# TensorE, ScalarE and VectorE in the text's order through the middle of a hybrid HGRN2/GLA trunk

## Chip, cores and metric

The kernel runs on one core of a Trainium2 chip. The metric is the device time of one execution in microseconds; the profile adds the span from the first to the last instruction, the instructions of each engine and the transfers.

## The reference

One layer over a sequence of 1024 tokens and 1024 channels, float32, batch 1. A conditioning vector gives a shift, a scale and a gate by `c_act @ ada_w`; the normalised input is modulated and projected once:

```python
h = rms_norm(x, norm_w[l]) * (1.0 + scale[:, None, :]) + shift[:, None, :]
proj = h @ w_in[l]
hq, hf, hi, hz, gq, gk, gv, gz, ga, mg = jnp.split(proj, IN_OFFSETS, axis=-1)
y_h = hgrn2_branch(hq, hf, hi, hz, lb_all[l], hgrn_norm_w[l])
y_g = gla_branch(gq, gk, gv, gz, ga, gla_alpha_w[l], gla_alpha_b[l], gla_norm_w[l])
u_h = y_h @ w_branch[l, 0]
u_g = y_g @ w_branch[l, 1]
merged = mg[:, :, 0] * u_h + mg[:, :, 1] * u_g
x = x + gate[:, None, :] * (merged @ w_out[l])
```

Here `mg` has been put through a sigmoid. Both branches are gated linear recurrences over time, `S_t = diag(a_t) S_{t-1} + k_t v_t^T` and `o_t = S_t^T q_t`: HGRN2 with 8 heads (keys and values 128 wide), GLA with 4 heads (keys 128 wide, values 256). Each branch output is normalised and multiplied by a SiLU gate. A final RMS norm closes.

## The kernel before

Every large product is made of three matmuls: each float32 operand is split into a rounded part `hi` and a rest `lo`, and hi·hi, hi·lo and lo·hi are added in PSUM. A split is one ScalarE cast (L211, L202, L1270, L1293) and one VectorE subtraction behind it (L212, L203, L1271, L1294), both on 128x1024.

The text goes through these stages. The first part (conditioning, normalisation, the first half of a first group of projections) is already in the text's order. `front()` finishes the first group. Then `stream.go()` runs a list of 62 jobs: 14 jobs `Vjob` that make the GLA values (L1899, two half products by a seven-product scheme), gate and key jobs of GLA (`Feat`, L607), 14 `Vjob` for the HGRN values, two more `Feat`, and 24 `Feat` for HGRN, three to a head: q, f and z. `last_stages()` and `out_stage()` follow with the mixing gates (`mg`), the branch and output products (L1351, L1528).

A job is cut into units of six matmuls 128x512: a `Vjob` has 4, a `Feat` has 8. After each unit `go()` calls `ahead`, which loads and splits the weights of the next jobs if slots are free, and `weave`, which advances two side tracks:

- `side` holds the attention heads, one after another. A head is a generator that yields how many units to wait before its next piece; the wait is divided by `PACE` 1.08 for GLA and `PACE_H` 1.15 for HGRN.
- `back` holds preparation for later: GLA decay rates (`alpha_side`), sums of weights (`v_sums`, `prepare` with its four additions L1195, L1197, L1199, L1201 per block) and the output gate (`gate_side`, seven accumulations L1072).

One head's pieces, in the text's order: VectorE builds scaled copies of q and k (L658 to L661, called the X block below; ScalarE copies q at L657); two or three units later TensorE makes a first set of scores (L665); VectorE scales q, k and the decays (L667 to L670), masks the scores into `blk` (L676, L679, L680, L681 for each half), then L682, L684, L693 and L694, which the next scores need (L698). Behind L698 stand L700 to L704, five masked copies (L739, L740, L742) and two growth steps of L726, L727, L729; after some units the scores L756, L762, L767 and their growth step, the transposes L791, the state updates (L813 on TensorE, L817 and L819 on VectorE) and the outputs (L832, L834), each half of which is squared on ScalarE (L1002 for GLA, L1123 for HGRN) and scaled on VectorE (L1003, L1124). A GLA head ends with an inverse root: two matmul pairs (L979, L980), a logarithm (L981), an exponential (L982) and eight products on VectorE (L1017). The next head starts when the one before it has ended, an HGRN head not earlier than five units after its f job.

At the end of a job its PSUM result is taken out: SiLU by ScalarE and VectorE (L967, L968) for q, z and the GLA gates, two sigmoids and three VectorE operations (L1102 to L1104) for f. Near the end of `go()` two hooks prepare the next stage; one, `begin_2`, stands four units before the last job's end and splits the factors (L1270, L1271) and one pair of weights (L1293, L1294).

What sets the order of the work: a scheduler takes the instructions that the text emits. On each engine it issues the instruction that stands earliest in the text among those that it holds to be ready in a model of the machine; an instruction whose inputs are late is passed by later ones. `keep_in_program_order` pins single instructions, `high_priority` (used with `EVICT_FIRST` around the taking out of a `Vjob`) moves some forward, and `manual_schedule(engines=...)` makes the named engines issue everything emitted inside it in the text's order. Before the change it is open only for the first part, as `order`. SyncE and GpSimd, which issue the transfers, are left to the scheduler everywhere. SBUF tiles come from 46 slots (`Slots`), handed out as the text is traced.

```python
    def go(self, loads=2, preps=1):
        for i, job in enumerate(self.jobs):
            self.ahead(i, loads + 2 * job.more, 0)
            for u, _ in enumerate(job.run()):
                if job.calls(u):
                    self.ahead(i, loads + 2 * job.more, preps + (job.more if u else 0))
                if (n - i, u) in self.hooks:
                    self.hooks[n - i, u]()
                self.weave(1)
```

Of the kernel before, what the change touches and what calls it, by code (L numbers as in the profile page):

```python
# [89 lines left out]
def hybrid_trunk_kernel(  # L90
# [805 lines left out]
    stream = Stream()  # L896
# [1039 lines left out]
    def front():  # L1936
        alpha = [alpha_half(half) for half in range(2)]
        for i, _ in enumerate(first_group()):
            if i < 10 and i % 2 == 0:
                next(alpha[0], None)  # L1940
            if i == 15:
                for _ in make_ga(1):
                    pass
                load_wq(0, 0)
                load_wq(1, 0)
            elif i in (16, 17, 18, 20, 22):
                next(alpha[1], None)
            elif i == 19:
                stream.ahead(0, 0, 0)
        for n, z in enumerate(("12", "22")):  # L1950
            xq[z] = [hT[1, 2 * n + kk] for kk in range(2)]
        stream.back.append([alpha_side((2, 3)), 72, 1, 0])
        stream.back.append([v_sums(), 2, 1, 0])
        stream.back.append([prepare(), 4, 1, 0])
        stream.back.append([gate_side(), 4, 1, 0])
# [1 line left out]
    stream.hooks[2, 0] = begin  # L1957
    stream.hooks[1, 4] = begin_2
    front()
    stream.go()  # L1960
    S.free(*h_hi, *h_lo)
    lent = [dtile() for _ in range(2)]
    R.lend([pd for pds in lent[::-1] for pd in pds])
# [31 lines left out]
```

## Time and profile before

| what | value |
|---|---|
| time, median of 3 runs | 1176.97 us (1176.68 to 1178.28) |
| profiled execution: time, span | 1178.0 us, 1176.2 us |
| TensorE busy | 1156.2 us, 98% of the span, 8137 matmuls |
| VectorE, ScalarE, GpSimd busy | 849.6 us (72%), 589.5 us (50%), 125.0 us (11%) |
| granted TensorE clock | 0.996 |
| `Vjob` matmuls L1899 | 672, mean 393 ns |
| `Feat` matmuls L607 | 1632, mean 395 ns |

A matmul's duration in the profile is longer than the step from one to the next, because matmuls overlap; the idle time of TensorE tells whether it waits. Times in rows are counted from the span's start. In the span's order `go()` reaches from about 111 us (first L1899) to about 778 us (last L607).

### The profile page before, as it was taken

What the parts mean: (1) busy time and instruction counts of PE and PEld (TensorE: products, weight loads), DVE (VectorE), ACT (ScalarE), POOL (GpSimd) and SP (SyncE); (2) the same over time, 40 slices, a digit from 0 to 9 for tenths busy, and PEclk for the clock granted to TensorE, in tenths of its full rate; (3) what the DMA queues carried; (4) which work ended last, traced back from release to release, by engine and by line L of the source; (5) the groups of instructions that cost most, each with busy time, mean ns of one, the idle gap of its engine ahead of it and who ended that gap; (6) DMA issues with size and microseconds to landing.
All of it is one profiled execution on the core that took longest, in us unless ns stands there. A gap on an engine that the chain in (4) does not pass through costs nothing.

```text
span 1176.2 us, 20432 instructions
## 1 busy us (share of the span) xinstructions
PE 1156.2 (98%) x8137; PEld 953.1 (81%) x8137; DVE 849.6 (72%) x1347; ACT 589.5 (50%) x903; POOL 125.0 (11%) x261
## 2 busy tenths in 40 slices
PE   7999999999999999999999999999999999999997
PEld 5777888888888788888888878888888888888886
DVE  4754778567665946897897798795643866988994
ACT  4675464663465535433433425567543644534654
POOL 4121111000100212111111010001110000000000
PEclk8999999999999999999999999999999999999999
DMA  9846445255675856565555453247699846434523
GB/s 319 279 149 233 161 170 189 77 165 171 207 260 177 279 189 201 171 203 173 174 184 188 134 205 112 91 162 241 196 314 298 274 156 215 130 108 162 187 90 134
DMA packets 150802, 221.44 MB, mean 188 GB/s; under 512 B 9052, under 2 KB 107410, under 8 KB 150707
## 3 DMA queue, kind: packets, MB, share of 16 engines
q1 hardware_dynamic: 132114, 158.37, 43.2%
q0 software_dynamic: 18544, 61.76, 13.6%
q8 instruction: 64, 1.05, 0.4%
q14 instruction: 32, 0.25, 0.1%
q10 hardware_dynamic: 48, 0.01, 0.0%
HBM read 154.57 MB, written 65.54 MB: 187 GB/s over the span
## 4 chain that ended last, share of the span: by engine, by line
PE 64%; issue 25%; DVE 4%; POOL 3%; DMA 2%; ACT 1%; SPq 0%; POOLq 0%; DVEq 0%; ACTq 0%
PE pd L607 16%; PE pd L1899 11%; PE pd L1351 9%; PE sc_ps L1351 5%; PE pm L1351 4%; PE pd L1528 3%; PE pd L396 3%; PE sc_ps L1528 2%; PE pm L832 1%; PE pm L1528 1%; POOL ws L1203 1%; PE sc_ps L396 1%; PE pm L834 1%; PE pm L813 1%; DMA b<-qk 1%
## 5 line engine op out<-in xcount | busy, mean ns | idle before, releaser
L607 PE MATMUL pd<-b,b 128*128 128x512 f32 x1632 | 391.1, 395 | 0.2 <-DVE b L212 0.2
L607 PEld LDWEIGHTS pd<-b,b 128*128 128x128 f32 x1632 | 302.1, 188 | 64.3 <-DVE b L212 0.6
L1351 PE MATMUL pd<-b,b 128*128 128x512 f32 x720 | 169.8, 390 | 0.1
L1899 PE MATMUL pd<-b,b 128*128 128x512 f32 x672 | 157.5, 393 | 2.6 <-ACT b L211 1.2
L1351 PEld LDWEIGHTS pd<-b,b 128*128 128x128 f32 x720 | 134.8, 188 | 28.5 <-ACT pd L1334 0.5
L1899 PEld LDWEIGHTS pd<-b,b 128*128 128x128 f32 x672 | 125.3, 188 | 30.5 <-ACT b L211 1.6
L212 DVE TENSOR_TENSOR b<-b,b 128x1024 fp32r<-128x1024 f32 x78 | 94.3, 1221 | 35.0 <-ACT b L211 34.7
L1294 DVE TENSOR_TENSOR b<-b,b 128x1024 fp32r<-128x1024 f32 x56 | 68.4, 1225 | 68.5 <-ACT b L1293 54.4
L1293 ACT CAST b<-b 128x1024 fp32r<-128x1024 f32 x56 | 58.5, 1049 | 69.5 <-PE pm L1351 17.0
L211 ACT CAST b<-b 128x1024 fp32r<-128x1024 f32 x78 | 79.8, 1047 | 12.1 <-DMA v<-b 3.9
L1351 PE MATMUL sc_ps<-b,b 128*128 128x512 f32 x324 | 77.2, 390 | 0.0
L1270 ACT CAST b<-b 128x1024 fp32r<-128x1024 f32 x48 | 49.7, 1049 | 46.5 <-PE pd L1351 16.0
L1351 PE MATMUL pm<-b,b 128*128 128x512 f32 x300 | 71.1, 389 | 0.0
L1351 PEld LDWEIGHTS sc_ps<-b,b 128*128 128x128 f32 x324 | 60.7, 188 | 12.6
L1271 DVE TENSOR_TENSOR b<-b,b 128x1024 fp32r<-128x1024 f32 x48 | 58.0, 1226 | 17.0 <-ACT b L1270 11.5
L1351 PEld LDWEIGHTS pm<-b,b 128*128 128x128 f32 x300 | 56.3, 188 | 11.7
L718 ACT COPY xb<-b 128x512 f32<-128x512 f32 x48 | 29.7, 621 | 55.8 <-DVE b L700 18.9
L1203 POOL DMA_DIRECT2D ws<-b x64 | 34.8, 545 | 190.6 <-DVE b L1195 118.7
L203 DVE TENSOR_TENSOR b<-b,b 128x1024 fp32r<-128x1024 f32 (+1 forms) x37 | 35.9, 984 | 26.4 <-ACT b L202 26.3
L396 PE MATMUL pd<-b,b 128*128 128x512 f32 x192 | 51.9, 403 | 0.5 <-ACT b L202 0.4
L832 PE MATMUL pm<-scT,b 128*128 128x128 f32 x256 | 46.9, 275 | 0.5 <-DVE b L819 0.5
L396 PEld LDWEIGHTS pd<-b,b 128*128 128x128 f32 x192 | 34.3, 188 | 11.6 <-ACT b L202 1.5
(316 smaller groups left out, 1713.3 us busy)
## 6 DMA issues: line engine op xcount, KB each, us to landing
b<-in_w_in_dram SPq DMA_DIRECT2D x72, 512.0 KB, 4.1
ws<-b POOLq DMA_DIRECT2D x64, 256.0 KB, 3.6
b<-ws SPq DMA_DIRECT2D x32, 512.0 KB, 4.6
b<-in_x_dram SPq DMA_DIRECT2D x16, 512.0 KB, 4.2
b<-in_ada_w_dram SPq DMA_DIRECT2D x32, 256.0 KB, 6.5
v<-b POOLq DMA_DIRECT2D x32, 256.0 KB, 4.3
b<-v SPq DMA_DIRECT2D x16, 512.0 KB, 5.0
b<-fx SPq DMA_DIRECT2D x16, 512.0 KB, 4.6
```

The lines of the kernel that those rows point to most:

```text
L211: held(nc.scalar.copy(hi, src))
L212: nc.vector.tensor_sub(lo, src, hi.bitcast(F32))
L396: nc.tensor.matmul(accs[f], wg(a, d, f), b[d][:, half * 512:half * 512 + 512], start=(d == 0 and n == 0), stop=(d == KT - 1 and n == 2))
L607: nc.tensor.matmul(ps[th][0:w, :], a[:, k, 0:w], b[:, th * 512:(th + 1) * 512], start=(k == 0 and n == 0), stop=(k == KT - 1 and n == 2))
L832: nc.tensor.matmul(o, vch(ch)[:, vh * P:(vh + 1) * P], scT[:, ch, :], start=True, stop=(ch == 0))
L1270: nc.scalar.copy(hi, src)
L1271: nc.vector.tensor_sub(lo, src, hi.bitcast(F32))
L1293: nc.scalar.copy(hi, t)
L1294: nc.vector.tensor_sub(lo, t, hi.bitcast(F32))
L1351: nc.tensor.matmul(o, a[:, sl], c, start=(p in (1, 5) and kt == 0 and n == 0), stop=(kt == 3 and n == 2), skip_group_check=True)
L1528: nc.tensor.matmul(o, a, b, start=(p in (1, 5) and kt == 0 and n == 0), stop=(kt == 3 and n == 2), skip_group_check=True)
L1899: nc.tensor.matmul(st.bank[i], x_, w_, start=(p in (1, 5) and kk == 0 and a == 0 and n == 0), stop=(kk == 1 and a == 1 and n == 2), skip_g ...
```

## The change

The call of `stream.go()` is put into a `manual_schedule` region for the three compute engines. Everything that `go()` emits on them, jobs, splits, heads and back track, is issued there in the text's order. The set of instructions, their tiles and slots, and the freedom of SyncE and GpSimd stay as they are; where the region's instructions fall among those emitted before and after it is still the scheduler's choice.

```diff
@@ -1957,7 +1957,8 @@
     stream.hooks[2, 0] = begin
     stream.hooks[1, 4] = begin_2
     front()
-    stream.go()
+    with tc.manual_schedule(engines={mybir.EngineType.PE, mybir.EngineType.Activation, mybir.EngineType.DVE}):
+        stream.go()
     S.free(*h_hi, *h_lo)
```

## The prediction, made before the changed kernel ran

> **What bounds the kernel now.** I read the busy time of the engines in windows first, then TensorE's order in time, then VectorE's beside it, and last the groups for single durations. The window rows give busy us of TensorE, its weight loads, VectorE, ScalarE and GpSimd; the second row is the stretch that the change covers.
>
> ```profile
> 473.00:784.00 311.00, 309.92 (x3206) 257.65 (x3206) 259.37 (x504) 134.95 (x245) 33.48 (x62) 1.00 0.52 165
> 106.00:784.00 678.00, 673.44 (x5821) 559.93 (x5820) 514.81 (x905) 325.52 (x516) 80.60 (x149) 1.00 0.55 178
> ```
>
> TensorE idles 678.00 - 673.44 = 4.56 us there. Nothing but TensorE's waits can be won, so 4.56 us is the whole possible gain. VectorE is at 514.81/678 = 76%, in the HGRN part at 259.37/311 = 83%; ScalarE is at 48%.
>
> Is TensorE's order the text's already? The timeline of HGRN head 2:
>
> ```profile
> 550.74 8.46 PE L607 MATMUL pd<-b,b 128*128 128x512 f32 x36
> 559.12 1.31 PE L665 MATMUL sc_ps<-xb,b 128*32 128x80 f32 x64
> 560.37 5.73 PE L607 MATMUL pd<-b,b 128*128 128x512 f32 x24
> 566.03 0.89 PE L698 MATMUL sc_ps<-xb,b 128*32 128x48 f32 x64
> 566.85 9.81 PE L607 MATMUL pd<-b,b 128*128 128x512 f32 x42
> ```
>
> Six matmuls are a unit. The text's count: a head starts 5 units after its f job; the yields 3, 5 and 4+3, each unit taking off 1.15, put L665 two units later, L698 four after L665, L756 seven after L698, and the next L665 follows L832 by six. The rows show 36, 24 and 42 matmuls: 6, 4 and 7 units. TensorE stands in the text's order now, so for it the edit changes nothing but waits; what changes is the order of ScalarE and VectorE.
>
> **The change part by part.** No instruction, byte or tile is added or removed, and none moves to another queue. SyncE and GpSimd stay the scheduler's; their loads and stores are hidden by work one or more jobs ahead, and would cost their lateness if that lead were gone. What goes is that VectorE and ScalarE pass an instruction whose input is late. What stands behind it now waits with it: on VectorE the X block and the L212 of the next job's split, and behind these TensorE's L665, L698 and the next job's first matmuls. ScalarE I cost at nothing: its idle half covers the changed order, and if that cover is gone one cast of about the length of a split's VectorE part (1.2 us, row L212 below) shows. The lost priority for taking out `Vjob` results I also cost at nothing: in the text that copy stands right behind its matmuls, and another bank is being filled.
>
> VectorE in head 2 (start, duration), and the square on ScalarE that its second L1124 waits for:
>
> ```profile
> 549.81 0.65 DVE L658 TENSOR_TENSOR xb<-b,b 128x256 f32<-128x256 f32 x1
> 550.35 0.75 DVE L1124 SCALAR_TENSOR_TENSOR b<-pm,vec,b 128x512 f32<-128x512 f32 x1
> ...
> 552.30 0.73 DVE L1124 SCALAR_TENSOR_TENSOR b<-pm,vec,b 128x512 f32<-128x512 f32 x1
> ...
> 562.26 0.30 DVE L679 COPY_PREDICATED blk<-mask,sc_ps 128x96 f32<-128x96 int32 x1
> 562.43 0.28 DVE L676 TENSOR_TENSOR blk<-sc_ps,eye 128x128 f32<-128x128 f32 x1
> ...
> 564.23 0.43 DVE L694 TENSOR_TENSOR xb<-xb,tot 128x256 f32<-128x256 f32 x1
> ...
> 567.24 0.27 DVE L701 TENSOR_TENSOR tot<-tot 128x64 f32<-128x64 f32 x1
> 567.54 0.28 DVE L702 TENSOR_TENSOR tot<-tot 128x64 f32<-128x64 f32 x1
> ...
> 572.50 1.22 DVE L212 TENSOR_TENSOR b<-b,b 128x1024 fp32r<-128x1024 f32 x1
> 573.64 0.69 DVE L726 TENSOR_TENSOR b<-b,tot 128x512 f32<-128x512 f32 x1
> ```
>
> ```profile
> 551.02 0.60 ACT L1123 ACTIVATE b<-pm 128x512 f32<-128x512 f32 x1 [1.19 <-PE pm L834]
> ```
>
> - *Fill lost.* Between 549.81 and 552.30 VectorE did L658, L659 and L667 around the first L1124: 2.49 - 0.66 = 1.83 us of later work in time that the text's order leaves idle. There the second L1124 starts at 551.02 + 0.60 + 0.06 = 551.7 instead of 552.30, so 1.83 - 0.6 = 1.2 us is net loss.
> - *Neighbours that depend.* L676 of one half follows L679 of the other after 0.17 us; L702, which reads what L701 wrote, follows after 0.30 us at the same length. The text puts L676, L679, L680, L681 of a half in a row, each on the last one's result: 6 such gaps at 0.13 to 0.15 us are 0.9 us, three more (L659-L660, L684-L693, L693-L694) 0.4 us. By L694 that is 1.3 us, and with three gaps among the masked copies 1.75 us by L212.
> - *Growth before the split.* In the text L212 stands behind the second growth step's L726 and L729, in the trace ahead of them: 0.7 us.
>
> One place of the Trainium skill speaks against the second item. VectorE: DVE Perf Modes, section "The DRAIN you can't avoid", says that eight chained copies took the same time with a semaphore after each as without, so that dependence costs nothing extra. The rows here disagree (0.17 against 0.30 us); by the page the sum would lose the second item, and I go by the rows.
>
> Deadlines: L694 is due at L698, the L212 at the first lo·hi matmul of the job, four matmuls after its start. L694 ends at 564.66, due 566.03: 1.37 us spare, 1.2 + 1.3 = 2.5 needed. L212 ends at 573.72; the job starts 30 matmuls after 566.85, at (9.81 - 0.28)/42 = 0.227 us each at 573.65, due 574.55: 0.83 spare, 1.2 + 1.75 + 0.7 = 3.65 needed. The second contains the first: head 2 loses 2.8 us. The other heads, by their L212 and the same matmuls (the row of head 4; heads lie 42.76 us apart):
>
> ```profile
> 487.69 1.22 DVE L212 TENSOR_TENSOR b<-b,b 128x1024 fp32r<-128x1024 f32 x1
> ...
> 527.82 1.23 DVE L212 TENSOR_TENSOR b<-b,b 128x1024 fp32r<-128x1024 f32 x1
> ...
> 614.11 1.22 DVE L212 TENSOR_TENSOR b<-b,b 128x1024 fp32r<-128x1024 f32 x1
> ...
> 657.37 1.22 DVE L212 TENSOR_TENSOR b<-b,b 128x1024 fp32r<-128x1024 f32 x1
> ```
>
> ```profile
> 652.37 9.81 PE L607 MATMUL pd<-b,b 128*128 128x512 f32 x42
> ```
>
> Due times 489.0, 531.8, 617.3 and 660.1; spare 0.1, 2.7, 2.0 and 1.5. Heads 1, 3 and 4 lose 0.9, 1.7 and 2.2. Head 0 follows a GLA head, has no L1124 in its way and has its growth step done before L212: only 1.75 needed, loss 1.65. In heads 5 and 6 the accumulations of the gate, which now slip in early, go back to their place behind L212; I take these two at no change (bounds 0 and 2.8 each).
>
> Head 7: `begin_2` emits three splits of 1.13 us on VectorE (3.4 us) right before the X block; the trace has them after it.
>
> ```profile
> 772.12 0.67 DVE L661 TENSOR_TENSOR xb<-xb,b 128x256 f32<-128x256 f32 x1
> ```
>
> ```profile
> 775.85 1.31 PE L665 MATMUL sc_ps<-xb,b 128*32 128x80 f32 x64
> ```
>
> Spare 3.06 us, needed 3.4 + 1.2: loss 1.6. HGRN sum: 1.65 + 0.9 + 2.8 + 1.7 + 2.2 + 1.6 = 10.85 us.
>
> GLA heads. Head 1's X block runs 50 us ahead of its place now, as filling:
>
> ```profile
> 199.68 0.64 DVE L658 TENSOR_TENSOR xb<-b,b 128x256 f32<-128x256 f32 x1 [4.13 <-PE sc_ps L762]
> ...
> 248.22 2.77 DVE L1017 TENSOR_TENSOR b<-b,b 128x256 f32<-128x256 f32 x8 [4.16 <-ACT b L982]
> 250.90 1.28 DVE L968 TENSOR_TENSOR b<-b,pd 128x512 f32<-128x512 f32 x2
> ```
>
> ```profile
> 252.00 1.31 PE L665 MATMUL sc_ps<-xb,b 128*32 128x80 f32 x64
> ```
>
> ```profile
> L659 DVE TENSOR_TENSOR xb<-b,b 128x512 f32<-128x512 f32 x12 | 10.4, 867 | 0.0
> L661 DVE TENSOR_TENSOR xb<-xb,b 128x256 f32<-128x256 f32 x12 | 7.7, 643 | 0.2
> ```
>
> In the text it stands behind the last L1017 and the job's L968, which end at 252.18, and takes 0.64 + 0.87 + 0.87 + 0.64 = 3.0 us: ready at 255.2, L665 due at 252.00, loss 3.2 us. Heads 2 and 3 have the same tail in the values stage; between nothing and 3.2 each I take 2.5, near the measured one. Sum 8.2 us. Head 0 and the first values stage I take at nothing: their VectorE work has no L1017 ahead of it and their splits are emitted a job and a half early; a single X block late would be 3.0.
>
> The waits there now (4.56 us) I leave in: most are at splits whose place in the text is late too. Sum: 10.85 + 8.2 = 19.05 us on the profiled execution's 1178.0 (span 1176.2 and 1.8 around it), 1197.0; the median lies 1.03 lower, so 1196.0.
>
> **The rivals.** *Faster.* Passing is also what makes the present waits: a filler takes VectorE just before the instruction that TensorE waits for. If the text's pacing suffices and two thirds of the 4.56 us go, the time is about 1174; it decides if the X blocks and L212 come earlier than my sums say, by more than the spares. Against it: the spares are 0.1 to 2.7 us, and every filler of head 2 was work that is due anyway. *No change.* Waits trade places: 1177. *Dependence is free.* Without the second item heads 0, 1 and 3 fit, 2 and 4 lose 1.1 and 0.4, head 7 1.6: 3.1 + 8.2 = 11.3, 1188. This is what the page's rule gives; the rows speak against it. *Blocking spreads.* ScalarE's casts wait behind logarithms and squares too, the heads 5 and 6 and the first stage lose as much as head 2, and GLA heads lose twice: 8 x 2.8 + 3 x 6.4 = 41.6 at the end (1218.6), some 1211 in the middle. For it: an in-order engine adds up its waits; against it: ScalarE is half idle, VectorE regains its lag between L756 and L832.
>
> **How the numbers follow.** Likeliest, 1189 to 1204: 0.45, at 1196. Dependence free, 1180 to 1189: 0.15. Spreading, above 1204: 0.16. No change, within 0.2% (2.35 us, about what a measurement of this kernel can tell): 0.12. Faster, at least 1172.4 by the bound: 0.12. For 8 in 10 the range goes from 1176, which leaves out the faster case and a part of no change, to 1210 with the lower half of spreading. Slower 0.76, same 0.12, faster 0.12.
>
> **What would show it.** Right: TensorE's rows keep 36, 24 and 42 matmuls between the scores; its waits grow at L665 (from VectorE L661), at L698 (L694) and at job starts (L212), most in heads 2 and 4 and in GLA heads 1 to 3; L676 to L681 stand in a row at 0.3 us; L658 of GLA head 1 comes after 250. Wrong: TensorE idle at or under 4.56 us; or waits mostly from ScalarE or from transfers; or another count of matmuls between the scores.

## The result and the profile after

The changed kernel took 1218.09 us (1216.71 to 1218.55), the kernel before 1177.62 us on the same chip: ratio of the means 1.0335, 95% interval 1.0308 to 1.0361. It is 40.5 us slower, where 19 were predicted. The profiled execution took 1218.55 us. Below, a time stands for the median of undisturbed executions, and e4_first and e9_wide have no undisturbed trace.

The core's span and granted clock, then the two window rows that answer to those of before (busy us of TensorE, weight loads, VectorE, ScalarE, GpSimd, then granted clock, DMA share, GB/s):

```profile
core 0: 1216.8 us, clock 0.986
```

```profile
473.00:784.00 311.00, 301.11 (x2901) 246.75 (x2901) 254.56 (x475) 118.39 (x218) 39.67 (x72) 0.99 0.52 167
106.00:784.00 678.00, 647.73 (x5398) 532.43 (x5397) 498.71 (x848) 290.81 (x469) 80.07 (x147) 0.98 0.52 169
```

TensorE now idles 678.00 - 647.73 = 30.3 us in a stretch where it idled 4.56 (the same work now lasts until about 822 us). The clock fell too, from 0.996 to 0.986. Between 106 and 1150 us the clock records show half speed for 3.41 us at 256.7, 263.5 and 748.2, and for 6.83 us at 335.2 and 413.7. What TensorE waits for between 100 and 830 us, the five largest entries of the view of waits (us in total, times, longest):

```profile
PE pd L607 <- ACT b L211: 6.9, 5, 3.7
PE sc_ps L665 <- issue: 6.2, 3, 3.1
PE sc_ps L665 <- DVE xb L661: 5.5, 4, 4.0
PE pm L791 <- DVE b L726: 2.3, 1, 2.3
PE sc_ps L698 <- DVE xb L694: 1.9, 3, 1.1
```

"Issue" means that the profile shows nothing that TensorE waited for. But each of the three L665 of that entry starts 0.1 us after the last L661 of its X block ends (at 182.78, 262.48 and 414.43 us), so the late X blocks account for 6.2 + 5.5 = 11.7 us. The waits at L665, L698 and at job starts were expected. Not expected: 6.9 us go to ScalarE's cast L211, and single waits reach 4.0 us where no loss was to be over 3.2.

A wait is not yet a loss, because TensorE may have been ahead. So I also use a **lag**: the start of the k-th wide matmul of a line (L1899, L607, L1351, L1528) in one trace, less the start of the k-th of that line in the trace of before. Its growth over each stretch gives the place of the loss, in us (the columns add up to the last, but for rounding; G are GLA heads, H HGRN heads):

| kernel | at 108 us | first values | G0 | G1 | G2 | G3 | H0 | H1 | H2 | H3 | H4 | H5, H6 | H7 | rest | end |
|---|---|---|---|---|---|---|---|---|---|---|---|---|---|---|---|
| predicted | 0 | 0 | 0 | 3.2 | 2.5 | 2.5 | 1.65 | 0.9 | 2.8 | 1.7 | 2.2 | 0 | 1.6 | 0 | 19.05 |
| after | -1.5 | 2.0 | 1.5 | 9.3 | 6.7 | 7.4 | 2.2 | 1.2 | 2.5 | 2.3 | 1.9 | 3.2 | 2.0 | 0 | 40.6 |
| e1_pe | -1.4 | 0.5 | 0.9 | 1.2 | 0 | 3.9 | 0.3 | 0 | 0 | 0 | 0 | 0.5 | 0 | -0.3 | 5.8 |
| e2_act | 0.1 | 0 | 0 | 1.8 | 0.9 | 2.5 | 0.1 | 0 | 0.4 | 0 | 0.8 | 1.4 | 1.3 | -0.4 | 8.9 |
| e3_dve | -0.1 | 0.1 | 1.5 | 5.4 | 3.2 | 3.0 | 1.8 | 1.1 | 2.5 | 2.2 | 1.9 | 2.4 | 2.0 | -0.4 | 26.7 |
| e6_x | -1.4 | 2.0 | 1.5 | 10.2 | 3.4 | 5.5 | 2.2 | 1.2 | 2.5 | 2.3 | 2.0 | 3.3 | 2.2 | -0.4 | 36.5 |
| e8_spread | -1.4 | 2.0 | 1.1 | 9.3 | 5.7 | 6.3 | 1.0 | 0 | 1.4 | 1.2 | 0.8 | 2.1 | 1.5 | -0.4 | 30.7 |
| e10_alpha | -0.7 | 2.0 | 2.4 | 0.6 | 5.3 | 7.4 | 2.2 | 1.2 | 2.5 | 2.3 | 1.9 | 3.2 | 2.1 | -0.4 | 32.0 |
| e11_rest | -1.3 | 2.1 | 1.5 | 8.7 | 2.5 | 7.2 | 2.2 | 1.2 | 2.5 | 3.8 | 1.9 | 3.3 | 2.1 | -0.2 | 37.4 |
| e13_wide | -0.3 | 2.0 | 1.5 | 9.1 | 6.3 | 7.4 | 2.2 | 1.2 | 2.5 | 2.3 | 2.0 | 3.2 | 2.0 | -0.4 | 41.0 |
| e14_near | -1.8 | 2.0 | 2.0 | -0.7 | 2.7 | 5.0 | 1.0 | 0 | 1.4 | 1.2 | 0.8 | 3.7 | 1.5 | 0.8 | 19.4 |
| e18_vec_only | -0.5 | 0.1 | 1.9 | -0.7 | 0.1 | 1.3 | 0.9 | 0 | 1.4 | 1.2 | 0.8 | 0.5 | 1.5 | -0.4 | 8.0 |

The HGRN heads are close to what was predicted; the GLA heads lost 23.4 us instead of 8.2. The worst place is the end of GLA head 0. ScalarE's timeline there (start, duration, idle before):

```profile
240.52 1.05 ACT L202 CAST b<-b 128x1024 fp32r<-128x1024 f32 x1 [5.73 <-DVE b L1010]
241.59 1.28 ACT L951 ACT_TABLE_LOAD   x1
242.88 2.01 ACT L951 ACTIVATE b<-b 128x1024 f32<-128x1024 f32 x2
244.91 1.28 ACT L967 ACT_TABLE_LOAD   x1
246.20 1.09 ACT L967 ACTIVATE b<-pd 128x512 f32<-128x512 f32 x2
247.31 1.28 ACT L981 ACT_TABLE_LOAD   x1
248.60 1.27 ACT L981 ACTIVATE b<-pm,eps_t 128x512 f32<-128x512 f32 x2
249.89 1.28 ACT L982 ACT_TABLE_LOAD   x1
251.18 1.06 ACT L982 ACTIVATE b<-b 128x1024 f32<-128x1024 f32 x1
252.26 1.28 ACT L954 ACT_TABLE_LOAD   x1
253.55 1.15 ACT L954 ACTIVATE b<-b,ones 128x1024 f32<-128x1024 f32 x1
254.61 1.03 ACT L211 CAST b<-b 128x1024 fp32r<-128x1024 f32 x1
```

ScalarE does not idle from 240.52 to 254.61: five table loads of 1.28 us and five functions, from the jobs and from both side tracks, stand in a row, with the cast for the next weights last. VectorE and TensorE beside it:

```profile
252.27 1.43 DVE L1017 TENSOR_TENSOR b<-b,b 128x256 f32<-128x256 f32 x4 [4.15 <-ACT b L982]
...
259.49 0.64 DVE L658 TENSOR_TENSOR xb<-b,b 128x256 f32<-128x256 f32 x1
```

```profile
255.69 1.25 PE L607 MATMUL pd<-b,b 128*128 128x512 f32 x4 [3.69 <-ACT b L211]
...
262.58 1.55 PE L665 MATMUL sc_ps<-xb,b 128*32 128x80 f32 x64 [1.97 <-issue]
```

VectorE stands 4.15 us in front of L1017 with work behind it that is ready. Before, it stood there about as long (4.16 us, the L1017 row of the prediction), but the next head's X block was already done by then, and so were its L667 to L670, which now follow L665 (264.09 to 266.79 us). Before:

```profile
203.13 0.61 DVE L667 TENSOR_TENSOR b<-b,b 128x256 f32<-128x256 f32 x1
...
205.60 0.63 DVE L670 TENSOR_TENSOR b<-b 128x256 f32<-128x256 f32 x1
```

### The profile page after: what moved, and what is told of

Its sections match the earlier page's. It is cut to its first block, busy times and chain, and to the rows that moved or that the text cites. A ratio compares the mean times of both kernels' runs of the same rounds, so it can differ in the third digit from the quotient of the medians.

```text
span 1216.8 us, 20435 instructions
## 1 busy us (share of the span) xinstructions
PE 1170.7 (96%) x8137; PEld 958.7 (79%) x8137; DVE 868.0 (71%) x1347; ACT 583.2 (48%) x900; POOL 126.3 (10%) x261
## 4 chain that ended last, share of the span: by engine, by line
issue 62%; PE 25%; POOL 8%; DMA 2%; DVE 1%; ACT 1%; SPq 0%; POOLq 0%; ACTq 0%; DVEq 0%
PE pd L1351 9%; PE sc_ps L1351 5%; PE pm L1351 4%; PE pd L1528 3%; POOL ws L1203 3%; PE sc_ps L1528 2%; POOL v L1789 1%; PE pm L1528 1%; DMA b<-in_ada_w_dram 1%; POOL yh L904 1%; DMA b<-in_x_dram 1%; POOL gate L1423 1%; POOL yg L904 1%; DMA gate<-b 1%; POOL qk L367 1%
## 5 line engine op out<-in xcount | busy, mean ns | idle before, releaser
L607 PE MATMUL pd<-b,b 128*128 128x512 f32 x1632 | 398.4, 399 | 10.0 <-ACT b L211 6.9
L607 PEld LDWEIGHTS pd<-b,b 128*128 128x128 f32 x1632 | 304.1, 190 | 79.7 <-ACT b L211 9.2
L1351 PE MATMUL pd<-b,b 128*128 128x512 f32 x720 | 170.0, 390 | 0.1
L1899 PE MATMUL pd<-b,b 128*128 128x512 f32 x672 | 161.3, 398 | 4.1 <-DVE b L212 1.5
L1351 PEld LDWEIGHTS pd<-b,b 128*128 128x128 f32 x720 | 134.8, 188 | 28.4 <-ACT pd L1334 0.5
L1899 PEld LDWEIGHTS pd<-b,b 128*128 128x128 f32 x672 | 127.2, 191 | 34.0 <-DVE b L212 2.6
L212 DVE TENSOR_TENSOR b<-b,b 128x1024 fp32r<-128x1024 f32 x78 | 94.0, 1220 | 35.1 <-ACT b L211 34.6
L211 ACT CAST b<-b 128x1024 fp32r<-128x1024 f32 x78 | 79.7, 1047 | 14.5 <-DVE b L212 9.0
L1351 PE MATMUL sc_ps<-b,b 128*128 128x512 f32 x324 | 77.1, 389 | 0.0
L1351 PE MATMUL pm<-b,b 128*128 128x512 f32 x300 | 71.1, 389 | 0.0
L1351 PEld LDWEIGHTS sc_ps<-b,b 128*128 128x128 f32 x324 | 60.7, 188 | 12.6
L1351 PEld LDWEIGHTS pm<-b,b 128*128 128x128 f32 x300 | 56.3, 188 | 11.7
L396 PE MATMUL pd<-b,b 128*128 128x512 f32 x192 | 51.9, 403 | 0.5 <-ACT b L202 0.4
L832 PE MATMUL pm<-scT,b 128*128 128x128 f32 x256 | 46.8, 275 | 0.0
L202 ACT CAST b<-b 128x1024 fp32r<-128x1024 f32 (+1 forms) x37 | 31.2, 853 | 26.1 <-DVE b L1010 13.7
```

Of the source, the lines that this page charges most:

```text
L211: held(nc.scalar.copy(hi, src))
L212: nc.vector.tensor_sub(lo, src, hi.bitcast(F32))
L396: nc.tensor.matmul(accs[f], wg(a, d, f), b[d][:, half * 512:half * 512 + 512], start=(d == 0 and n == 0), stop=(d == KT - 1 and n == 2))
L607: nc.tensor.matmul(ps[th][0:w, :], a[:, k, 0:w], b[:, th * 512:(th + 1) * 512], start=(k == 0 and n == 0), stop=(k == KT - 1 and n == 2))
L1351: nc.tensor.matmul(o, a[:, sl], c, start=(p in (1, 5) and kt == 0 and n == 0), stop=(kt == 3 and n == 2), skip_group_check=True)
L1899: nc.tensor.matmul(st.bank[i], x_, w_, start=(p in (1, 5) and kk == 0 and a == 0 and n == 0), stop=(kk == 1 and a == 1 and n == 2), skip_g ...
```

## The experiments

Line numbers shift where an edit adds lines: L698 is L706 in e6_x, L709 in e14_near, L701 in e8_spread, e7_fill and e13_wide.

**Which engine's order costs.** Each of three kernels gives one engine the text's order.

```diff
-    with tc.manual_schedule(engines={mybir.EngineType.PE, mybir.EngineType.Activation, mybir.EngineType.DVE}):
+    with tc.manual_schedule(engines={mybir.EngineType.PE}):            # e1_pe
+    with tc.manual_schedule(engines={mybir.EngineType.Activation}):    # e2_act
+    with tc.manual_schedule(engines={mybir.EngineType.DVE}):           # e3_dve
```

> TensorE alone in the text's order, VectorE and ScalarE the scheduler's. Theory (VectorE's and ScalarE's order cost the 40.5 us, TensorE's own order nothing): 1176 to 1180 us, ratio 0.998 to 1.002, granted clock 0.996. Rival (TensorE's order, in which some 30 matmuls of the region stand elsewhere than before, costs by itself): above 1185 us.

Measured: 1184.7 us, 1.0050 (1.0034 to 1.0066). Between the two; my theory's 1176 to 1180 was missed. The lag is mostly at GLA head 3: counting wide matmuls in TensorE's order, L665 of every head but this one stands where it stood; here it comes after 1296 instead of 1305, nine matmuls or 2 us sooner, ahead of its X block. Before, and e1_pe (the window of this view ends inside L665):

```profile
395.26 1.31 PE L665 MATMUL sc_ps<-xb,b 128*32 128x80 f32 x64
```

```profile
397.96 1.25 PE L665 MATMUL sc_ps<-xb,b 128*32 128x80 f32 x60 [2.00 <-DVE xb L661]
```

> ScalarE alone in the text's order. Theory (ScalarE's Exp, Ln and table loads in the text's order hold up the L211 cast of the next split at the end of GLA head 0): a TensorE wait of 3 to 4 us near 252 us and half a clock window or two behind it, some 1.6 us more at GLA head 3, in all +8 us: 1186 us. Rival, as in the prediction (ScalarE's order costs nothing): 1177 us.

Measured: 1185.5 us, 1.0045 (1.0030 to 1.0061). The total is as expected, the place is not: near 250 us TensorE's wait for the cast is only 0.51 us. ScalarE's order alone does not make the 3.69 us wait; that VectorE, left to the scheduler, worked around it is the likely reason.

> VectorE alone in the text's order. Theory (its part is the larger: waits of about 18 us and some 9 us of half-clock windows behind those of 2 us and more): 1204 us. Rival 1 (the prediction's sum, waits alone): 1196 us. Rival 2 (the loss needs both engines in the text's order, as the one would fill what the other leaves late): under 1190 us.

Measured: 1204.1 us, 1.0202 (1.0179 to 1.0224), with 3.4 us lost to the clock (two windows of 3.41 us at half speed), not 9. VectorE's order is some 60% of the loss. The three alone give 0.50 + 0.45 + 2.02 = 2.97%, of 3.35.

**Which stretch.** The region is closed, or opened, at the first HGRN job.

```diff
+            text = ExitStack()
+            text.enter_context(tc.manual_schedule(engines={...}))    # e4_first; e5_hgrn: at the job below
             for i, job in enumerate(self.jobs):
+                if n - i == 24:
+                    text.close()
```

> All three engines in the text's order, but only up to the first HGRN job; from there the scheduler's. Theory (from the trace of after: waits of 18.8 us and half-clock windows worth 10 us lie before 473 us): 1204 to 1207 us, granted clock 0.987 to 0.99. Rival, the prediction's sizes (8.2 us for the GLA heads, the rest in the HGRN heads): 1186 us.

> All three engines in the text's order from the first HGRN job on, the scheduler's before. By the prediction's head losses (sum 10.85 us): 1189 us, no TensorE wait over 2.5 us. By the lag of after behind before, which grows by 15 us from 480 us to the end: 1193 us. Rival (the HGRN heads lose only because the part before left VectorE late): under 1183 us.

Measured: e4_first 1203.2 us, 1.0200 (1.0175 to 1.0225); e5_hgrn 1193.9 us, 1.0145 (1.0123 to 1.0167). The halves add up (3.45%), and the HGRN heads lose about the same with or without an earlier lateness (17.2 us of lag in e5_hgrn, 15.3 in the changed kernel; heads 1 to 4 agree to 0.1 us). By the ratios the second half costs some 17 us where the prediction had 10.85, the first some 24 where it had 8.2.

**X block ahead of L1017.** In GLA heads 1 to 3 the X block is written after the previous head's split L202 and before its L980.

```diff
-        yield from inverse_root(rst, sq[0], 256)
+        root = inverse_root(rst, sq[0], 256)
+        yield next(root)
+        if h < 3:
+            x_block(qk["q", h + 1], alphas[h + 1])
+        yield from root
```

> The changed kernel, with the X block (L657 to L661) of GLA heads 1 to 3 written ahead of the previous head's L982 and L1017, where VectorE idles 4 us; nothing else moved. Theory (the X block stands in VectorE's text order behind L1017, and that behind ScalarE's Ln and Exp with their table loads): the waits at L665 of 2.0, 4.0 and 3.1 us go, and with them the half-clock windows at 263, 335 and 414 us, worth 8.5 us: 1201 to 1206 us. Rival 1 (waits go, the clock does not follow): 1209 us. Rival 2 (something else is late for L665 or the next matmul, such as q's load or the split): over 1212 us.

Measured: 1214.1 us, 1.0310 (1.0291 to 1.0329): in the range of rival 2. The waits at L665 of GLA heads 1 to 3 went, but in heads 1 and 3 TensorE now waits one step later, since L667 to L694 still stand behind L1017:

```profile
271.77 0.89 PE L706 MATMUL sc_ps<-xb,b 128*32 128x48 f32 x64 [2.43 <-DVE xb L702]
...
421.25 0.89 PE L706 MATMUL sc_ps<-xb,b 128*32 128x48 f32 x64 [2.91 <-DVE xb L702]
```

**Keeping TensorE busy in the wait.** Matmuls that nothing uses stand ahead of L665 of GLA heads 2 and 3, narrow ones in e7_fill, wide ones in e9_wide; e13_wide is e9_wide again.

```diff
+        for _ in range(FILL.get(me, 0)):      # e7_fill: {3: 36, 4: 30}; e9_wide, e13_wide: {3: 15, 4: 12}
+            nc.tensor.matmul(sc_ps[1][:, 464:512], ones, ident[:, 0:48], start=True, stop=True)        # e7_fill
+            nc.tensor.matmul(sc_ps[1], h_hi[0][:, 0:P], h_hi[0][:, 0:512], start=True, stop=True)      # e9_wide
```

> The changed kernel, with 36 and 30 small matmuls of 128x48 (into columns that nothing reads) ahead of L665 of GLA heads 2 and 3, where TensorE waits 4.0 and 3.1 us. Theory (the half clock follows a long wait of TensorE, not the place or the work after it): the 6.83 us windows at 335 and 414 us go, the data-bound lateness stays, 3.4 us each: 1211 us, granted clock 0.991. Rival (the clock falls for another reason): 1218 us or more with the windows still there.

Measured: 1229.0 us, 1.0440 (1.0421 to 1.0460), the rival, and more. The fill itself (two matmuls in the profile for each of the text) and a window inside it:

```profile
332.21 11.20 PE L665 MATMUL sc_ps<-ident,ones 128*128 128x48 f32 x72
```

```profile
340.00:344.00 4.00, 4.00 (x36) 3.91 (x40) 0.00 (x0) 0.00 (x0) 0.00 (x0) 0.50 0.06 25
```

TensorE is busy without a gap, yet the clock halves: 72 narrow matmuls with their weight loads (one per matmul, 3.91 us of 4.00) take 156 ns each and do not hold it.

> The changed kernel, with 15 and 12 matmuls of 128x512 (227 ns each, into the scores' bank, which L665 overwrites) ahead of L665 of GLA heads 2 and 3, in place of the small ones of e7_fill. Theory (the clock follows the columns that stream through the array, which narrow matmuls hardly supply and a wait not at all): no half-clock window at 335 and 414 us, the lateness of 4.0 and 3.1 us stays: 6.8 us off 1218, 1211 us, clock 0.991. Rival (the narrow L665 that follows, or the place itself, lowers the clock): windows stay, 1218 us or more.

> e9_wide again, for its trace (its three quiet runs gave 1218 us at a granted clock of 0.992, against 0.986 of the changed kernel). If the clock loss at 335 and 414 us is a cost by itself: no half-clock window there and the gain lost elsewhere, at a place that the trace names. If TensorE at half clock only filled a time in which VectorE was late anyway: a wait at the next L698 of 2 to 4 us each that the changed kernel has not, and the same lag of some 25 us at 480 us.

Measured: e9_wide 1218.1 us, 1.0330 (1.0303 to 1.0356); e13_wide 1219.3 us, 1.0333 (1.0310 to 1.0356). At these two places the clock is held, and the time does not move. The changed kernel first, then e13_wide:

```profile
336.00:340.00 4.00, 2.83 (x65) 2.59 (x66) 3.90 (x8) 1.19 (x3) 0.00 (x0) 0.50 0.74 228
```

```profile
414.53 2.36 PE L665 MATMUL sc_ps<-xb,b 128*32 128x80 f32 x64 [3.09 <-issue]
416.82 8.83 PE L1899 MATMUL pd<-b,b 128*128 128x512 f32 x30
425.58 0.89 PE L698 MATMUL sc_ps<-xb,b 128*32 128x48 f32 x64
```

```profile
336.00:340.00 4.00, 3.36 (x73) 2.58 (x73) 3.93 (x6) 0.43 (x2) 0.00 (x0) 1.00 0.77 279
```

```profile
416.43 7.13 PE L1902 MATMUL pd<-b,b 128*128 128x512 f32 x30
426.08 0.89 PE L701 MATMUL sc_ps<-xb,b 128*32 128x48 f32 x64 [2.53 <-DVE xb L697]
```

At half clock the 30 matmuls before L698 of GLA head 3 took 8.83 us and L698 did not wait; at full clock they take 7.13 and L698 waits 2.53 us for VectorE, with a new half-clock window at 427.2 us behind that wait. At GLA head 2 L698 waits in neither kernel; there e13_wide gives the gain back a little later, in two waits for ScalarE's copies out of a `Vjob` (L1785, L1782 in the changed kernel):

```profile
353.90 1.66 PE L1902 MATMUL pd<-b,b 128*128 128x512 f32 x6 [0.84 <-ACT b L1785]
356.28 1.66 PE L1902 MATMUL pd<-b,b 128*128 128x512 f32 x6 [0.72 <-ACT b L1785]
```

So at these two places, 13.7 of the 23.9 us at half clock, the slow clock cost next to nothing of its own: it filled time in which another engine was late. For the windows at 256, 263 and 748 us this was not tried.

**Dependent neighbours.** The two halves of L676 to L681 and of L739, L740 alternate in the text.

```diff
+        for z in range(2):
+            TT(bzs[z], pcs[z][:, :, 0:32], bc(eye32.unsqueeze(1), [4, 32]), M)
+        for bv, px in zip(bvs, pxs):
             cpr(bv[:, :, :, 1:4], bc(mk[:, :, :, 0:5:2], [4, 8, 3]), px[:, :, :, 0:5:2])
+        for bv, px in zip(bvs, pxs):
             cpr(bv[:, :, :, 2:4], bc(mk[:, :, :, 1:6:4], [4, 8, 2]), px[:, :, :, 1:6:4])
...
```

> The changed kernel, with the two halves of L676 to L681 and of L739, L740 interleaved in the text, so that no instruction of these reads what the one before wrote. Theory of the prediction (0.30 us a step where each depends on its neighbour, 0.17 where not; about 1.2 us sooner at L694 and L212): the waits at L698 (1.9 us) go and those at L607 behind L212 shrink, 3 to 8 us: 1210 to 1215 us. Rival (VectorE has the time there anyway, the waits come from places further back): 1217 to 1219 us.

Measured: 1209.2 us, 1.0271 (1.0255 to 1.0286), 8.9 us less than the changed kernel by the medians, 7.5 by the ratios. HGRN head 2, after and e8_spread (x2 is a pair, one of each half):

```profile
590.75 0.28 DVE L676 TENSOR_TENSOR blk<-sc_ps,eye 128x128 f32<-128x128 f32 x1
591.07 0.30 DVE L679 COPY_PREDICATED blk<-mask,sc_ps 128x96 f32<-128x96 int32 x1
591.40 0.30 DVE L680 COPY_PREDICATED blk<-mask,sc_ps 128x64 f32<-128x64 int32 x1
591.74 0.30 DVE L681 COPY_PREDICATED blk<-mask,sc_ps 128x32 f32<-128x32 int32 x1
...
592.98 0.97 DVE L682 TENSOR_TENSOR b<-b,b 128x768 f32<-128x768 f32 x1
```

```profile
586.12 0.48 DVE L678 TENSOR_TENSOR blk<-sc_ps,eye 128x128 f32<-128x128 f32 x2
586.52 0.46 DVE L680 COPY_PREDICATED blk<-mask,sc_ps 128x96 f32<-128x96 int32 x2
...
587.47 0.96 DVE L685 TENSOR_TENSOR b<-b,b 128x768 f32<-128x768 f32 x1
```

The same eight instructions take 592.98 - 590.75 = 2.23 us in a row and 587.47 - 586.12 = 1.35 us alternating. The two halves also lie in different PSUM tiles, but that is not the reason: the four copies L739 and L740, which read one PSUM tile, went from 1.00 to 0.73 us (599.97 to 600.97 us, and 594.46 to 595.19 in e8_spread). HGRN heads 0 to 4 get 1.1 to 1.2 us back each, heads 5 and 6 together 1.1, head 7 0.5.

**The alpha track on ScalarE.**

```diff
-        stream.back.append([alpha_side((2, 3)), 72, 1, 0])
+        stream.back.append([alpha_side((2, 3)), 64, 1, 0])
```

> The changed kernel, with the alpha track (L951 to L958) started at unit 64 in place of 72, so that its Exp, Ln and table loads stand ahead of L202 and L981 of GLA head 0 on ScalarE and no longer between L982 and the next L211. Theory (ScalarE's text order makes the 3.7 us wait at 252 us): that wait and its half-clock window go, some 5 to 7 us: 1211 to 1213 us. Rival (VectorE's L1017 block holds the split up as long): 1216 to 1218 us.

Measured: 1209.8 us, 1.0263 (1.0240 to 1.0285), 8.3 us less than the changed kernel, more than expected. GLA head 1 loses 0.6 us instead of 9.3 (head 0 loses 2.4 instead of 1.5), and L211 follows L982 at once. The gain is not ScalarE's alone: the edit also moves the track's VectorE instructions, of which two L955 stand among the L1017 in the changed kernel, and e3_dve, with ScalarE free, still loses 5.4 us at this head.

```profile
248.32 1.06 ACT L982 ACTIVATE b<-b 128x1024 f32<-128x1024 f32 x1
249.28 1.04 ACT L211 CAST b<-b 128x1024 fp32r<-128x1024 f32 x1
```

**L1017 later.** On e6_x's text, L1017 is taken off the head's generator and put 14 units later; e12_all adds e8_spread and e10_alpha; e14_near takes 4 units and lets the next head start so that every L665 is at the changed kernel's matmul.

```diff
+        def scale():
             for half in range(4):
...
+        stream.rest.append([scale(), 0, PACE, stream.units + (14 if h < 3 else 0)])    # e14_near: 4
...
+        if h:
+            yield 6                                                                     # e14_near: 5.5
         yield from attention(...)
```

> As e6_x, and L1017 of GLA heads 0 to 2 written 14 units later on a track of its own, behind the next head's L698 block; L665 keeps its place on TensorE. Theory (VectorE stands 4 us before L1017, which waits for ScalarE's L982, and everything behind it is late: X block, L212, L694): the lag of 22.7 us that after gathers between 241 and 480 us falls to 6 to 10 us, of which the wait at 252 us is most: 1202 to 1206 us. Rival (VectorE's work between L665 and L698 is itself too long for 5 units): as e6_x, 1212 to 1215 us.

> e8_spread, e10_alpha and e11_rest together, still all three engines in the text's order. If the three causes add up (L1017 behind L982 12 to 16 us, alpha on ScalarE 5 to 7 us, dependent neighbours 9 us): 1187 to 1193 us. Rival (they overlap, as one lateness hides the other): 1197 us or more.

> e12_all with L1017 only 4 units later and the next head starting 5.5 units after, so that L665 stands at the same matmul of TensorE's order as in the changed kernel. Theory (e12_all's stall of 2.8 + 1.8 us at L980 and its 6.83 us half-clock window near 386 us came from the shift by one unit, which put four L211 casts ahead of L202): stall and window go, 8 us less: 1187 to 1190 us. Rival (L1017 falls back between L665 and L698 and holds L694 up): 1194 us or more.

Measured: e11_rest 1214.6 us, 1.0302 (1.0280 to 1.0324), missed, the rival's time; e12_all 1196.3 us, 1.0145 (1.0123 to 1.0166), near its rival; e14_near 1196.9 us, 1.0144 (1.0129 to 1.0159), its rival. Head 2 loses 2.5 us instead of 6.7, but e6_x, with L1017 in its old place, already had 3.4. And without moving L1017, e6_x, e8_spread and e10_alpha took off 4.0, 8.9 and 8.3 us, which would add up to 1196.9: that moving L1017 gains anything by itself is not shown. e11_rest and e12_all shift the heads by one unit, and four casts fall ahead of L202 of head 2, on which TensorE's L980 and a half-clock window hang; e14_near mends that and pays at L698 and behind it. The four casts on ScalarE in e12_all, and TensorE in e14_near:

```profile
377.24 3.90 ACT L211 CAST b<-b 128x1024 fp32r<-128x1024 f32 x4 [1.95 <-PE pd L1920]
```

```profile
408.69 0.89 PE L709 MATMUL sc_ps<-xb,b 128*32 128x48 f32 x64 [2.01 <-DVE xb L705]
```

**Longer leads.** e14_near with the X block of GLA head 0 four units sooner, of each HGRN head one unit sooner, and the gate's L1072 at half the rate.

```diff
-    vjobs[0][12].begins = first_head
+    vjobs[0][11].begins = first_head
-        yield lead
+        yield lead + extra   # 4.3 for GLA head 0, 1.15 for HGRN: L665 stays
-            start_side(hgrn_attention(h), 5, PACE_H)
+            start_side(hgrn_attention(h), 4, PACE_H)
...
-            yield 1          # gate_side
+            yield 2
```

> e14_near, with the X block of GLA head 0 four units earlier, of each HGRN head one unit earlier (L665 and all behind it where they were) and the gate's L1072 at one per two units in place of one per unit. Theory (what is left of the loss is the short lead of the X block in the text and L1072 in VectorE's order ahead of L726): the waits at L665 of 1.1, 0.5, 0.3 and 0.7 us and those of 1.3 and 2.0 us near 725 to 737 us go: 4 to 6 us less than e14_near. Rival (each goes over to L698 or the next L607): 0 to 2 us less.

Measured: 1195.1 us, 1.0126 (1.0108 to 1.0143): the rival. The L665 wait of GLA head 0 (1.13 us) became 1.37 us at a `Vjob` matmul. HGRN heads 5 and 6 lose nothing any more (3.7 us in e14_near), which fits L1072 as their cause (their X blocks came sooner too), but head 7 now loses 4.0 us instead of 1.5.

**The same text with other engines fixed** (e14_near's text; e16_vec_free fixes TensorE and ScalarE, e17_free nothing, e18_vec_only VectorE).

> e14_near's text, TensorE and ScalarE in the text's order, VectorE the scheduler's. Theory (what is left of the loss in e14_near, 17 us, is VectorE's standing order alone: each repair only moves its lateness to the next place): 1177 to 1181 us. Rival (TensorE and ScalarE lose some 5 and 6 us by themselves, as in e1_pe and e2_act, and the text's edits did not mend that): 1186 to 1192 us.

> e14_near's text with all engines the scheduler's. Theory (the scheduler finds these places itself, so that the edits of the text bring nothing without the order): 1176 to 1180 us, within 0.3% of before. Rival (the earlier alpha track and the interleaved halves help the scheduler too): 1172 to 1175 us.

> e14_near's text, VectorE alone in the text's order. Theory (VectorE's order carries the rest): 1188 to 1195 us, 10 us or more under e3_dve's 1204. Rival (the edits mend only what ScalarE's order did): 1200 us or more.

Measured: e16_vec_free 1184.0 us, 1.0047 (1.0031 to 1.0062); e17_free 1180.8 us, 1.0020 (1.0007 to 1.0032); e18_vec_only 1185.4 us, 1.0057 (1.0037 to 1.0076). e17_free is at the edge of its theory, and its rival is out: the edits bring nothing without the order. e16_vec_free lies between theory and rival. e18_vec_only did better than its theory: VectorE's order alone costs 0.57% in this text where it cost 2.02% in the old one, so the edits did mend VectorE's part. The parts give 0.47 + 0.57 = 1.04%, or 0.84 if the 0.20% of e17_free, which is in both, is counted once; the whole is 1.44. So some 5 to 7 us arise only where all three engines are held, presumably as none can give way for another (the intervals leave these 5 to 7 us uncertain by 3 or 4). By the lags much of it lies in GLA heads 2 and 3, which lose 7.7 us in e14_near, 2.5 in e16_vec_free and 1.4 in e18_vec_only; what makes it there stays open. No version ran faster than the kernel before.

## Why the prediction was right or wrong

Right in sign, wrong in size: 19 us predicted, 40.5 measured, outside the range.

- *TensorE keeps its place.* Right for HGRN head 2 (36, 24 and 42 matmuls between L832, L665, L698 and L756, as the rows below show) and for every L665 but two. HGRN head 7's comes after nine matmuls of the next stage; GLA head 3's came 2 us sooner, and e1_pe loses 3.9 us there; "for it the edit changes nothing but waits" was drawn from one head.

```profile
579.49 8.46 PE L607 MATMUL pd<-b,b 128*128 128x512 f32 x36
588.38 1.31 PE L665 MATMUL sc_ps<-xb,b 128*32 128x80 f32 x64 [0.44 <-DVE xb L661]
589.63 5.73 PE L607 MATMUL pd<-b,b 128*128 128x512 f32 x24
595.80 0.89 PE L698 MATMUL sc_ps<-xb,b 128*32 128x48 f32 x64 [0.44 <-DVE xb L694]
596.61 7.09 PE L607 MATMUL pd<-b,b 128*128 128x512 f32 x30
604.05 1.20 PE L607 MATMUL pd<-b,b 128*128 128x512 f32 x4 [0.34 <-ACT b L211]
605.76 2.13 PE L607 MATMUL pd<-b,b 128*128 128x512 f32 x8 [0.51 <-DVE b L212]
```

- *HGRN heads 0 to 4 and 7.* 10.85 us predicted, 12.1 measured, each within 0.6 us. The deadline method holds, and not by luck alone: less the 1.15 us a head that alternating took off (0.88 and 0.27, rows of e8_spread), the same sums leave heads 0 to 4 and 7 losses of 0.5, 0, 1.7, 0.5, 1.0 and 1.6 us, and e8_spread shows 1.0, 0, 1.4, 1.2, 0.8 and 1.5.
- *Dependent neighbours.* 1.3 us by L694 and 1.75 by L212 predicted; taking away most of it returned 1.1 to 1.2 in HGRN heads 0 to 4, and 7.5 to 8.9 in all; the six gaps put at 0.9 us measured 2.23 - 1.35 = 0.88. The rival "dependence is free" is out: 0.32 to 0.34 us a step in a row, 1.35/8 = 0.17 alternating. The sentence of the Trainium skill (VectorE: DVE Perf Modes, "The DRAIN you can't avoid") did not say that it is free: it says that a semaphore after each of eight chained copies cost nothing extra over one after the last, and no run here tests that.
- *Fill lost, 1.2 us, and the growth step, 0.7.* Not tried apart. VectorE does idle 0.98 us in front of the second L1124 of head 2 now (at 580.40 us).
- *Heads 5 and 6 at no change.* Wrong: 3.2 us, within the bounds given. The gate's L1072 stands ahead of L726 now, and L791 waits 2.32 us for L726; e15_lead, with L1072 at half the rate and the X blocks sooner, loses nothing at these heads.
- *GLA heads 1 to 3 at 8.2.* The step that failed most: 23.4 (9.3, 6.7 and 7.4 where 3.2, 2.5 and 2.5 stood). I counted one late X block a head. But the X block was only the first in line: L667 to L670, which in heads 1 and 2 had also run early as filling, now stand behind L1017 and the X block too and push L676 to L694 and the next L212 back (e6_x moved the X block alone, and in heads 1 and 3 TensorE waited at L698 instead). In head 1 the alpha track comes on top: moving it gives back 8.7 of the 9.3 us. In head 2 moving the X block gives back 3.3 of the 6.7. Of head 3's 7.4 us 5.0 are left in e14_near, and what makes them stays open, TensorE's own order apart (e1_pe).
- *ScalarE at nothing.* Wrong: "its idle half" is a mean. From 240.52 to 254.61 it has no idle time at all, TensorE waits 3.69 us for the L211 at its end, and e10_alpha, which only moves the alpha track, won 8.3 us. Where VectorE is free the same ScalarE order costs 1.8 us at this place, so much of the cover that I named was VectorE's freedom, which the edit also took away.
- *First values stage and GLA head 0 at nothing.* 3.5 us; GLA head 0's L665 waits 1.13 us for its X block. The -1.5 us at 108 us is no gain of the change: e17_free, without a region, has -1.2 there and e13_wide, with it, -0.3, so single traces differ by this much ahead of `go()`.
- *The rival "blocking spreads"*, with 41.6 us at its end, is what happened in size. I gave it 0.16 because ScalarE is half idle. Its split was off: GLA heads lost 7.8 each instead of 6.4, heads 5 and 6 1.6 each instead of 2.8. That its sum comes so close to 40.5 is luck in part, as these errors cancel.
- *A TensorE clock of 1.00 throughout* was taken for granted in every due time. At the two places tried this did not matter.

## What to carry to other kernels

Before an engine is put into a fixed order, list for each of its instructions what would stand behind it while it waits, and read idle time in the window of that wait, not in the mean of the span. An order fixed on several engines at once can cost more than on each alone (1.44% against 0.84 to 1.04 here), presumably since the slack that one engine gave another goes too. In a fixed order let neighbours on VectorE be independent: alternating two halves was worth some 8 us here for a few moved lines.

## What the runs showed of the hardware

**The clock follows half a window of idleness.** The clock records change on a fixed grid of 3.41 us. I divided 17 traces (all but those of e4_first and e9_wide, before left out) from 106 to 1150 us into these windows and added up TensorE's waits in each. Each of the 31 full-clock windows in which TensorE waited 1.80 us or more was followed by one at half clock; none with 1.58 or less was, save behind e7_fill's narrow matmuls; between the two five were and seven were not. The Trainium skill (TensorE: Matmul & The Clock Gate, "Why this matters for your kernels") advises against idle gaps over some 3 us. The grid agrees with the free-running window of its Part 1; the gap that suffices is shorter here, if it lies in one window.
